# Products that nothing reads in the routing, and another order of two squares in the head

## The chip, the cores and the metric

One core of a Trainium2 chip runs the whole program in one launch. Its engines work side by side, each through its own list of instructions in order, and wait for each other on semaphores: TensorE (PE) multiplies matrices, VectorE (DVE), ScalarE (ACT) and GpSimd (POOL) work element by element, SyncE (SP) issues most of the DMAs. The metric is device time in microseconds (us). TensorE runs at one of two clock levels, 2.4 GHz or 1.2 GHz, which the profile's rows show as a granted clock of 1.00 or 0.50.

## The reference

The input x has 512 rows of 1024. Two blocks follow each other, all in float32:

```python
x = first_block(x, c, ...)      # gated linear attention and pooling, then hier_moe
return second_block(x, ...)     # a gated delta rule layer, swiglu, a stick-breaking attention, swiglu

def hier_moe(h, w_rg, w_re, w_e_in, w_e_out):
    t = h.reshape(-1, D)
    pg = softmax(t @ w_rg)                      # 4 groups: the best one
    gp, gi = top_k(pg, 1)
    le = (t @ w_re).reshape(-1, 4, 8)           # 8 experts in that group: the best two
    le = take_along_axis(le, gi)
    ew, ei = top_k(softmax(le), 2)
    weights = gp * ew / sum(ew)
    ...                                         # 32 experts: y = sum of weight * (silu(t wi_a) * (t wi_u)) @ wo
    return y

# end of first_block, start of second_block
x = x + gt_m * hier_moe(modulate(rmsnorm(x, norm2_g), sh_m, sc_m), ...)
x = rmsnorm(x, final_norm_g)
hn = rms_norm(x, attn_norm[0])
proj = hn @ w_in                                # gdn_mixer: q, k, v, z, b, a
```

gt_m, sh_m and sc_m are columns of silu(c) @ w_ada + b_ada. In gdn_mixer the projected q, k and v go through a short convolution and silu; then, in chunks of 64 rows, a triangular system is solved for each head.

## The kernel before

The data stand transposed: xT has 8 tiles of 128 features by 512 rows. A product of full precision is made of three: the operand is split into a high and a low part (ah and al, by ACT and DVE), the weight as well (whi by ACT, wlo by DVE or POOL), and ah*whi, al*whi and ah*wlo are summed (the function mm3). Every instruction goes through one helper, so all rows of the profile name line 231; they are told apart by the names of their tiles.

**The routing** (moe, lines 1305 to 1500 or so) chooses experts for every row. PE makes small products: with sel (which expert each row has), to count and rank the rows (tile names lA<-sel,lsr); with oh, a one-hot matrix, to list for each pair of experts which rows belong to it (lA<-vals,oh). Between them DVE makes a long chain of small operations, one after the other. From the list DVE makes indices, POOL gathers the rows by indirect DMA, DVE scales them (moex<-moex,sums, the function scaled), PE transposes them (lA<-cst,moex), ACT and DVE modulate them (operand), and the expert products (mm<-slot,moex) begin. In the gaps of this chain the code puts the last two column blocks of the ada product (mm<-wraw,sil, then lC<-cst,ms to turn the row into columns, which DVE adds into modT and modP). The generator gate_gen (lines 1340 to 1350) makes these in steps, and the code calls go(n), n steps, at chosen places: go(4) ahead of everything, go(2) after the products with sel, go(1) after the indices, go(100) after the gathers were issued. Ahead of the expert loop stands a block that runs only if some expert has more rows than its place holds; its branch reads a number that DVE made (line 1622).

**The head** (lines 1721 to 1745) joins the last experts' results into xT, tile by tile (k from 0 to 7), and starts the next stage's first projection two tiles behind. Per tile: PE transposes the experts' results (lA<-to,ylast), DVE adds them into xT, ACT makes ah, DVE makes al, and two sums of squares are kept for two norms: st1, of x, with DVE's addition nacc<-nacc,nsq, and st2, of x times a gain, with POOL's addition of the same name. The helper norm_add (lines 638 to 647) issues the square on ACT and the addition behind it at once. In the program's order ACT makes ah of tile k, the square of st1 for tile k-1, and the square of st2 for tile k; DVE makes xT of k, the addition of k-1, and al of k:

```python
into_x(ps, k)                                          # DVE xT
s.nc.scalar.activation(hh[:, k], x, AF.Copy, ...)      # ACT ah
if k:
    s.norm_add(st1, s.xT[:, k - 1])                    # ACT nsq, DVE nacc, of the tile before
V.scalar_tensor_tensor(out=hl[:, k], ...)              # DVE al
s.norm_add(st2, x, fg[:, k:k + 1], G)                  # ACT nsq, POOL nacc
```

Behind the head PE sums the two norms over the partitions (lA<-nacc,ones), ACT makes R from them, DVE Rc, and each projected piece is scaled by Rc into xm.

**The stage after it** (gdn, from line 1747) is written as generators: projections, convolution (kF, qF, vf: DVE adds three shifted products to one of ACT's), silu on ACT, transposes on PE (lC<-cst,vf), and the triangular solve on DVE, in which 30 steps of a product sub<-mt and an addition mt<-mt,sub follow each other. A planner decides the order in which the generators' steps are emitted: it keeps an emulated time for every engine, from costs written into the program, and asks which lane has work that an engine could start. The times run on from what was emitted in the head, so another order there gives it another start.

Of the kernel before, what the change touches and what calls it, by code (L numbers as in the profile page):

```python
# [12 lines left out]
F = mybir.dt.float32  # L13
# [381 lines left out]
class Kern:  # L395
# [242 lines left out]
    def norm_add(s, st, x, scale=1.0, eng=None):  # L638
        n = st["n"]
        if st["first"]:  # L640
            s.nc.scalar.activation(st["acc"][:, :n], x, AF.Square, scale=scale)
            st["first"] = False
        else:
            q = s.tp.tile([P, 512], F, name="nsq", tag="nsq", bufs=2)
            s.nc.scalar.activation(q[:, :n], x, AF.Square, scale=scale)
            (eng or s.nc.vector).tensor_tensor(out=st["acc"][:, :n], in0=st["acc"][:, :n], in1=q[:, :n], op=OP.add)

# [659 lines left out]
    def moe(s):  # L1307
# [32 lines left out]
        def gate_gen():  # L1340

            for j in (10, 11):
                ps = s.mm_tile()
                for _ in s.ada_gen(j, ps):
                    yield
                ms = s.tp.tile([P, 256], F, name="ms", tag="hF", bufs=2)
                S.activation(ms, ps[:, 0:256], AF.Copy)
                yield
                for _ in s.columns_gen(j, ms):
                    yield  # L1350
# [3 lines left out]
        go(4)  # L1354
        Rt = sm("Rt2", [4])
# [100 lines left out]
        with s.aside():  # L1456
# [3 lines left out]
            skip_runtime_bounds_check_because="the result of a comparison: 0 or 1")  # L1460
        tp_ = s.la_tile([P, 5, NP])
# [195 lines left out]

        warm = sm("warm", [1])
# [47 lines left out]
    def head(s, part, into_x):  # L1706
# [9 lines left out]
        first = [s.mm_tile() for _ in range(2)]  # L1716
        for k in range(KT + 2):
            if k < KT:
                ps = part(k)
                x = s.xT[:, k]  # L1720
                with s.aside():
                    into_x(ps, k)
                    s.nc.scalar.activation(hh[:, k], x, AF.Copy, scale=fag[:, k:k + 1])
                    if k:
                        s.norm_add(st1, s.xT[:, k - 1])
                    V.scalar_tensor_tensor(out=hl[:, k], in0=x, scalar=fag[:, k:k + 1], in1=hh[:, k].bitcast(F),
                                           op0=OP.mult, op1=OP.subtract)
                    s.norm_add(st2, x, fg[:, k:k + 1], G)
                    if k == KT - 1:
                        s.norm_add(st1, x)  # L1730
# [792 lines left out]
```

## Time and profile before

| | us |
|---|---|
| median of 3 runs | 2022.58 (2020.38 to 2023.29) |
| profiled execution | 2029.18 |
| its span in the profile | 2027.4 |
| PE busy | 1949.6, 96% of the span |
| DVE, ACT, POOL busy | 981.0, 756.3, 373.8 |
| mean granted clock of TensorE | 0.973 |

The profile is of one execution; the span leaves out some time around it, and the runs are timed without a profile. A row of a timeline gives start and duration; in brackets stand the idle time of the engine just before and the work whose end released it. Consecutive instructions of one engine and kind are one row with their count (x32); a float32 product counts as two records. The stretches of this program are, in us from the span's start: the first block's mixer up to 325, the routing to 348, the experts to 604.5, the head to 637, the delta rule layer to 1041, and then the rest.

### The profile page before, as it was taken

What the parts mean: (1) busy time and instruction counts of PE and PEld (TensorE: products, weight loads), DVE (VectorE), ACT (ScalarE), POOL (GpSimd) and SP (SyncE); (2) the same over time, 40 slices, a digit from 0 to 9 for tenths busy, and PEclk for the clock granted to TensorE, in tenths of its full rate; (3) what the DMA queues carried; (4) which work ended last, traced back from release to release, by engine and by line L of the source; (5) the groups of instructions that cost most, each with busy time, mean ns of one, the idle gap of its engine ahead of it and who ended that gap; (6) DMA issues with size and microseconds to landing.
All of it is one profiled execution on the core that took longest, in us unless ns stands there. A gap on an engine that the chain in (4) does not pass through costs nothing.

```text
span 2027.4 us, 26781 instructions
## 1 busy us (share of the span) xinstructions
PE 1949.6 (96%) x10717; PEld 1468.5 (72%) x10717; DVE 981.0 (48%) x1612; ACT 756.3 (37%) x1188; POOL 373.8 (18%) x305
## 2 busy tenths in 40 slices
PE   7999997999998997999999999999999989999999
PEld 4776775444445776888788888888888768888887
DVE  3445344334446788545554433445665554433432
ACT  3443322222225653444343312234666542322322
POOL 0513202111105442122121101101221221100110
PEclk8988997999998998999999999999999999999999
DMA  8213286999962323111223333323211123323322
GB/s 300 90 45 115 74 297 224 419 411 401 410 246 57 110 79 96 45 27 42 94 85 94 102 94 94 104 83 104 73 63 58 47 73 104 94 94 97 95 89 73
DMA packets 175367, 268.86 MB, mean 133 GB/s; under 512 B 24300, under 2 KB 148456, under 8 KB 162696
## 3 DMA queue, kind: packets, MB, share of 16 engines
q1 hardware_dynamic: 152784, 249.28, 35.6%
q10 hardware_dynamic: 19784, 13.40, 2.3%
q0 software_dynamic: 2672, 4.44, 0.6%
q8 instruction: 86, 1.41, 0.3%
q14 instruction: 41, 0.34, 0.1%
HBM read 263.41 MB, written 7.86 MB: 134 GB/s over the span
## 4 chain that ended last, share of the span: by engine, by line
PE 73%; DVE 5%; ACT 2%; issue 2%; POOL 1%; DMA 0%; ACTq 0%; POOLq 0%; DVEq 0%
PE mm L231 57%; PE lA L231 9%; PE lB L231 7%; DVE sub L231 1%; DVE xT L231 1%; PE lC L231 1%; DVE qF L231 1%; DVE mt L231 0%; ACT ah L231 0%; DVE kF L231 0%; POOL wlo L231 0%; DVE vf L231 0%; DVE wlo L231 0%; DVE al L231 0%; ACT whi L231 0%
## 5 line engine op out<-in xcount | busy, mean ns | idle before, releaser
L231 PE MATMUL mm<-ah,whi 128*128 128x512 f32 (+1 forms) x1232 | 502.8, 408 | 0.8 <-DVE xT L231 0.4
L231 PE MATMUL mm<-al,whi 128*128 128x512 f32 (+1 forms) x1232 | 487.5, 396 | 7.4 <-DVE al L231 7.3
L231 PE MATMUL mm<-ah,wlo 128*128 128x512 f32 (+1 forms) x1232 | 487.1, 395 | 0.8 <-DVE wlo L231 0.8
L231 DVE TENSOR_TENSOR wlo<-wraw,whi 128x1024 fp32r<-128x1024 f32 (+3 forms) x174 | 216.4, 1245 | 295.6 <-ACT whi L231 293.7
L231 ACT ACTIVATE whi<-wraw 128x1024 fp32r<-128x1024 f32 (+2 forms) x212 | 214.8, 1015 | 331.6 <-PE mm L231 178.6
L231 PEld LDWEIGHTS mm<-ah,whi 128*128 128x128 f32 (+1 forms) x1232 | 233.7, 190 | 61.1 <-issue 11.0
L231 PEld LDWEIGHTS mm<-al,whi 128*128 128x128 f32 (+1 forms) x1232 | 234.2, 190 | 57.8 <-DVE al L231 9.8
L231 PEld LDWEIGHTS mm<-ah,wlo 128*128 128x128 f32 (+1 forms) x1232 | 233.7, 190 | 54.1 <-DVE wlo L231 2.0
L231 POOL TENSOR_TENSOR sg<-sg,fR 128x512 f32<-128x512 f32 x44 | 57.0, 1296 | 525.6 <-ACT sg L231 525.6
L231 POOL TENSOR_TENSOR wlo<-wraw,whi 128x1024 fp32r<-128x1024 f32 x38 | 93.1, 2451 | 254.6 <-ACT whi L231 247.4
L231 PE MATMUL mm<-hidh,whi 128*128 128x512 f32 x352 | 139.2, 395 | 0.0
L231 PE MATMUL mm<-hidh,wlo 128*128 128x512 f32 x352 | 138.0, 392 | 0.0
L231 PE MATMUL mm<-hidl,whi 128*128 128x512 f32 x352 | 136.6, 388 | 0.0
L231 PE MATMUL mm<-slot,moex 128*32 128x512 f32 (+1 forms) x1024 | 117.9, 602 | 0.1
L231 ACT ACTIVATE moex<-lA,modP,g2P 128x128 f32<-128x128 f32 x64 | 27.6, 456 | 161.4 <-PE lA L231 146.0
L231 PEld LDWEIGHTS mm<-slot,moex 128*32 128x32 f32 x1024 | 31.7, 111 | 72.3 <-issue 64.7
L231 PEld LDWEIGHTS mm<-hidh,wlo 128*128 128x128 f32 x352 | 66.1, 188 | 15.5
L231 PEld LDWEIGHTS mm<-hidl,whi 128*128 128x128 f32 x352 | 66.1, 188 | 14.5
L231 PEld LDWEIGHTS mm<-hidh,whi 128*128 128x128 f32 x352 | 66.2, 188 | 13.0
L231 DVE TENSOR_TENSOR xT<-mm,xT 128x512 f32<-128x512 f32 x64 | 44.0, 687 | 55.6 <-PE mm L231 49.7
L231 ACT ACTIVATE hidh<-fu 128x512 fp32r<-128x512 f32 x44 | 27.8, 633 | 103.9 <-DVE fu L231 103.9
L231 DVE TENSOR_SCALAR moex<-lA,g2P,modP 128x128 f32<-128x128 f32 x64 | 25.3, 410 | 85.1 <-ACT moex L231 85.1
(552 smaller groups left out, 3115.4 us busy)
## 6 DMA issues: line engine op xcount, KB each, us to landing
slot<-in_w_e_in_dram SPq DMA_DIRECT2D x64, 1024.0 KB, 11.8
wraw<-in_w_gu_dram SPq DMA_DIRECT2D x88, 512.0 KB, 3.4
slot<-in_w_e_out_dram SPq DMA_DIRECT2D x32, 1024.0 KB, 13.0
wraw<-in_w_down_dram SPq DMA_DIRECT2D x40, 512.0 KB, 3.4
wraw<-in_w_ada_dram SPq DMA_DIRECT2D x32, 512.0 KB, 4.1
wraw<-in_gdn_w_in_dram SPq DMA_DIRECT2D x32, 512.0 KB, 3.8
wraw<-in_w_kv_dram SPq DMA_DIRECT2D x16, 512.0 KB, 3.4
wraw<-in_w_in_dram SPq DMA_DIRECT2D x14, 512.0 KB, 4.6
```

The lines of the kernel that those rows point to most:

```text
L231: r = f(*a, **k)
```

## The change

Three things are changed.

- gate_gen holds back the last step of column block 10 (the turning into columns is done, DVE's addition waits) until the first quarter of block 11's products has been issued, and one more go(1) puts that quarter ahead of the products with oh.
- A function busy(n) makes n products of the ones matrix (128x128, float32) with itself into a PSUM tile that nothing reads: 14 after go(4), 3 ahead of the products with oh, 5 ahead of the expert loop.
- In the head a new function square issues a square on ACT and hands back the addition, to be issued later. ACT now makes ah, the square of st1 and the square of st2, all of tile k; the addition of st1 for tile k is issued in tile k+1, between ah and al. The rest of the program stays, except that the planner gives the stage after the head another order.

```diff
--- before.py
+++ after.py
@@ -644,6 +644,18 @@
             q = s.tp.tile([P, 512], F, name="nsq", tag="nsq", bufs=2)
             s.nc.scalar.activation(q[:, :n], x, AF.Square, scale=scale)
             (eng or s.nc.vector).tensor_tensor(out=st["acc"][:, :n], in0=st["acc"][:, :n], in1=q[:, :n], op=OP.add)
+
+    def square(s, st, x, scale=1.0, eng=None):
+
+        n = st["n"]
+        if st["first"]:
+            st["first"] = False
+            s.nc.scalar.activation(st["acc"][:, :n], x, AF.Square, scale=scale)
+            return lambda: None
+        q = s.tp.tile([P, 512], F, name="nsq", tag="nsq", bufs=2)
+        s.nc.scalar.activation(q[:, :n], x, AF.Square, scale=scale)
+        return lambda: (eng or s.nc.vector).tensor_tensor(out=st["acc"][:, :n], in0=st["acc"][:, :n],
+                                                          in1=q[:, :n], op=OP.add)
 
     def rsqrt_(s, out, src, scale):
         s.nc.scalar.activation(out, src, AF.Ln, scale=scale, bias=s.eps)
@@ -1339,19 +1351,33 @@
 
         def gate_gen():
 
+            last = None
             for j in (10, 11):
                 ps = s.mm_tile()
                 for _ in s.ada_gen(j, ps):
                     yield
+                    if last:
+                        next(last)
+                        last = None
+                        yield
                 ms = s.tp.tile([P, 256], F, name="ms", tag="hF", bufs=2)
                 S.activation(ms, ps[:, 0:256], AF.Copy)
                 yield
-                for _ in s.columns_gen(j, ms):
-                    yield
+                last = s.columns_gen(j, ms)
+                next(last)
+                yield
+            next(last)
+
+        def busy(n):
+
+            ps = s.la_tile(lane="B")
+            for _ in range(n):
+                PE.matmul(ps[:, 0:P], s.ones, s.ones, start=True, stop=True)
 
         gg = gate_gen()
         go = lambda n=1: [next(gg, None) for _ in range(n)]
         go(4)
+        busy(14)
         Rt = sm("Rt2", [4])
         s.rsqrt_(Rt, p2[:, :, 0], 1.0 / D)
         lg = sm("lg", [4, 36])
@@ -1458,6 +1484,8 @@
         _, dyn = nc.values_load_multi_w_load_instructions(
             moi[0:1, 0:NP], engines=[ET.PE], min_val=0, max_val=1,
             skip_runtime_bounds_check_because="the result of a comparison: 0 or 1")
+        go(1)
+        busy(3)
         tp_ = s.la_tile([P, 5, NP])
         for i in range(2):
             h = slice(4 * i, 4 * i + 4)
@@ -1655,6 +1683,7 @@
                 ts_(out=over_, in0=over_, scalar1=-128.0, scalar2=0.0, op0=OP.add, op1=OP.max)
         s.aloof = False
 
+        busy(5)
         warm = sm("warm", [1])
         S.activation(warm, s.eps, AF.Silu)
         s.pairs.room += 1
@@ -1714,6 +1743,7 @@
         hh, hl = s.act_tiles()
         st1, st2 = s.norm_begin(), s.norm_begin()
         first = [s.mm_tile() for _ in range(2)]
+        add = lambda: None
         for k in range(KT + 2):
             if k < KT:
                 ps = part(k)
@@ -1721,13 +1751,13 @@
                 with s.aside():
                     into_x(ps, k)
                     s.nc.scalar.activation(hh[:, k], x, AF.Copy, scale=fag[:, k:k + 1])
-                    if k:
-                        s.norm_add(st1, s.xT[:, k - 1])
+                    add()
                     V.scalar_tensor_tensor(out=hl[:, k], in0=x, scalar=fag[:, k:k + 1], in1=hh[:, k].bitcast(F),
                                            op0=OP.mult, op1=OP.subtract)
-                    s.norm_add(st2, x, fg[:, k:k + 1], G)
+                    add = s.square(st1, x)
                     if k == KT - 1:
-                        s.norm_add(st1, x)
+                        add()
+                    s.square(st2, x, fg[:, k:k + 1], G)()
             if k > 1:
                 kk = k - 2
                 if kk % 4 == 0:
```

PE's list in the routing, before, behind the ada products of block 10 (mm<-wraw,sil), from the products with sel to the last ada products:

```order
L231 MATMUL lA<-sel,lsr 128x128
L231 MATMUL lA<-sel,lsr 128x96
L231 MATMUL lA<-sel,lsr 128x64
L231 MATMUL lA<-sel,lsr 128x32 x5
L231 MATMUL lC<-cst,ms 128x2 x4
L1458 TENSOR_LOAD moi
L231 MATMUL lA<-vals,oh_2666 128x80 x4
L231 MATMUL lA<-vals,oh_2672 128x80 x4
L231 MATMUL mm<-wraw,sil 32x256 x16
```

and now (lB is the tile that nothing reads, TENSOR_LOAD moi reads the flags for the expert loop):

```order
L231 MATMUL lB_2506<-ones 128x128 x14
L231 MATMUL lA<-sel,lsr 128x128
L231 MATMUL lA<-sel,lsr 128x96
L231 MATMUL lA<-sel,lsr 128x64
L231 MATMUL lA<-sel,lsr 128x32 x5
L231 MATMUL lC<-cst,ms 128x2 x4
L1484 TENSOR_LOAD moi
L231 MATMUL mm<-wraw,sil 32x256 x4
L231 MATMUL lB_2687<-ones 128x128 x3
L231 MATMUL lA<-vals,oh_2692 128x80 x4
L231 MATMUL lA<-vals,oh_2698 128x80 x4
L231 MATMUL mm<-wraw,sil 32x256 x12
```

Four of the sixteen last ada products moved ahead of the products with oh, and two groups of products with ones stand in between.

ACT's list at the end of the head, before, from ah of the seventh tile (k = 6) to the load of the table for R:

```order
L231 ACTIVATE ah<-xT,fag 128x512
L231 ACTIVATE nsq<-xT 128x512
L231 ACTIVATE nsq<-xT,vaT 128x512
L231 ACTIVATE whi<-wraw 128x1024
L231 ACTIVATE ah<-xT,fag 128x512
L231 ACTIVATE nsq<-xT 128x512
L231 ACTIVATE nsq<-xT,vaT 128x512
L231 ACTIVATE nsq<-xT 128x512
L218 ACT_TABLE_LOAD
```

and now:

```order
L231 ACTIVATE ah<-xT,fag 128x512
L231 ACTIVATE nsq<-xT 128x512
L231 ACTIVATE nsq<-xT,vaT 128x512
L231 ACTIVATE whi<-wraw 128x1024
L231 ACTIVATE ah<-xT,fag 128x512
L231 ACTIVATE nsq<-xT 128x512
L231 ACTIVATE nsq<-xT,vaT 128x512
L218 ACT_TABLE_LOAD
```

The two kinds of squares (nsq<-xT for st1, nsq<-xT,vaT for st2) stand alike in both. Before, the one for st1 is of the tile before the ah above it, and the last tile's follows at the end; now both are of the same tile as that ah.

DVE's list in the solve, before, from the scaled piece xm to the first vf (the convolution of v), over the fifth to the eighth pair of sub and mt:

```order
L231 TENSOR_TENSOR xm<-mm,Rc 128x512
L231 TENSOR_TENSOR sub<-mt 128x130
L231 TENSOR_TENSOR mt<-mt,sub 128x26x5
L231 TENSOR_TENSOR sub<-mt 128x150
L231 TENSOR_TENSOR mt<-mt,sub 128x25x6
L231 TENSOR_TENSOR sub<-mt 128x168
L231 TENSOR_TENSOR mt<-mt,sub 128x24x7
L231 TENSOR_TENSOR sub<-mt 128x184
L231 TENSOR_TENSOR mt<-mt,sub 128x23x8
L231 TENSOR_SCALAR qss<-lC 128x4
L231 TENSOR_SCALAR qss<-qss 128x4
L231 SCALAR_TENSOR_TENSOR vf<-xm,vbT,vf 128x512 x2
```

and now, over the same pairs:

```order
L231 SCALAR_TENSOR_TENSOR vf<-xm,vbT,vf 128x512
L231 MEMSET xm 128x3
L231 TENSOR_TENSOR xm<-mm,Rc 128x512
L231 TENSOR_TENSOR sub<-mt 128x130
L231 TENSOR_TENSOR mt<-mt,sub 128x26x5
L231 TENSOR_TENSOR sub<-mt 128x150
L231 TENSOR_TENSOR mt<-mt,sub 128x25x6
L231 TENSOR_TENSOR sub<-mt 128x168
L231 TENSOR_TENSOR mt<-mt,sub 128x24x7
L231 TENSOR_TENSOR sub<-mt 128x184
L231 TENSOR_TENSOR mt<-mt,sub 128x23x8
L231 SCALAR_TENSOR_TENSOR vf<-xm,vbT,vf 128x512 x2
```

The first vf, which stood after the eighth pair, now stands after the fourth, and the pairs of vf that follow are one addition further on.

## Rows read from the trace of the kernel before

**Rows 1.** The page: busy time by engine; the chain that ended last.

```profile
PE 1949.6 (96%) x10717; PEld 1468.5 (72%) x10717; DVE 981.0 (48%) x1612; ACT 756.3 (37%) x1188; POOL 373.8 (18%) x305
...
PE 73%; DVE 5%; ACT 2%; issue 2%; POOL 1%; DMA 0%; ACTq 0%; POOLq 0%; DVEq 0%
```

**Rows 2.** Stretch, length, busy of PE, PEld, DVE, ACT, POOL; clock, DMA share, GB/s.

```profile
348.00:604.50 256.50, 255.07 (x1927) 108.04 (x1928) 104.32 (x188) 67.10 (x129) 37.93 (x28) 0.99 0.94 381
...
604.50:632.50 28.00, 20.00 (x70) 13.29 (x68) 18.55 (x24) 17.13 (x27) 15.08 (x9) 0.90 0.13 34
...
737.00:800.00 63.00, 48.53 (x239) 38.70 (x239) 57.14 (x105) 19.53 (x25) 24.67 (x12) 0.89 0.30 82
```

**Rows 3.** Timeline, PE, routing: start, duration, products, [idle before, releaser].

```profile
325.96 1.93 PE L231 MATMUL mm<-wraw,sil 128*32 128x256 f32 x32
...
332.82 1.86 PE L231 MATMUL lA<-sel,lsr 128*128 128x128 f32 x8 [4.92 <-DVE sel L231]
...
338.56 1.90 PE L231 MATMUL lA<-vals,oh 128*128 128x80 f32 x8 [2.20 <-DVE oh L231]
...
340.39 3.55 PE L231 MATMUL mm<-wraw,sil 128*32 128x256 f32 x32
...
348.02 1.95 PE L231 MATMUL lA<-cst,moex 128*128 128x128 f32 x8 [2.45 <-DVE moex L231]
```

**Rows 4.** Stretches of the routing: length, busy PE, clock, DMA share, GB/s.

```profile
331.00:343.00 12.00, 7.98 (x52) 0.50 0.70 251
...
348.00:353.50 5.50, 5.48 (x28) 0.50 0.88 294
```

**Rows 5.** Timeline, PE, further on: products of 128x128 at full clock.

```profile
692.96 1.95 PE L231 MATMUL lB<-kF 128*128 128x128 f32 x16
```

**Rows 6.** Timeline, POOL and DVE, routing: first gather, scaling of gathered rows.

```profile
341.17 1.13 POOL L1491 DMA_INDIRECT moex<-x1d,src  x1 [5.02 <-DVE tk L231]
...
347.12 0.75 DVE L231 TENSOR_SCALAR moex<-moex,sums 128x1024 f32<-128x1024 f32 x1 [1.35 <-DVEq L1622]
```

**Rows 7.** Timeline, DVE, head.

```profile
608.10 0.75 DVE L231 SCALAR_TENSOR_TENSOR al<-xT,fag,ah 128x512 fp32r<-128x512 f32 x1 [0.79 <-ACT ah L231]
...
623.37 0.75 DVE L231 SCALAR_TENSOR_TENSOR xT<-lA,modT,xT 128x512 f32<-128x512 f32 x1
...
625.43 0.69 DVE L231 TENSOR_TENSOR nacc<-nacc,nsq 128x512 f32<-128x512 f32 x1 [1.31 <-ACT nsq L231]
...
626.70 0.74 DVE L231 SCALAR_TENSOR_TENSOR xT<-lA,modT,xT 128x512 f32<-128x512 f32 x1
...
628.75 2.05 DVE L231 TENSOR_TENSOR nacc<-nacc,nsq 128x512 f32<-128x512 f32 x1 [1.31 <-ACT nsq L231]
...
630.72 1.75 DVE L231 SCALAR_TENSOR_TENSOR al<-xT,fag,ah 128x512 fp32r<-128x512 f32 x1
```

**Rows 8.** Timeline, ACT and PE, head.

```profile
624.78 0.61 ACT L231 ACTIVATE nsq<-xT 128x512 f32<-128x512 f32 x1
...
636.77 0.69 ACT L231 ACTIVATE R<-lA,eps 128x512 f32<-128x512 f32 x1 [4.01 <-PE lA L231]
...
634.83 3.09 PE L231 MATMUL lA<-nacc,ones 128*128 128x512 f32 x4
```

**Rows 9.** Timeline, POOL, head.

```profile
609.28 1.29 POOL L231 TENSOR_TENSOR nacc<-nacc,nsq 128x512 f32<-128x512 f32 x1 [17.45 <-ACT nsq L231]
...
627.89 2.36 POOL L231 TENSOR_TENSOR wlo<-wraw,whi 128x1024 fp32r<-128x1024 f32 x1
...
630.21 1.72 POOL L231 TENSOR_TENSOR nacc<-nacc,nsq 128x512 f32<-128x512 f32 x1
```

**Rows 10.** Timeline, PE and DVE, solve of the next stage.

```profile
775.84 1.11 PE L231 MATMUL lC<-cst,vf 128*128 128x128 f32 x4 [8.88 <-ACT vf L231]
...
769.05 1.41 DVE L231 SCALAR_TENSOR_TENSOR vf<-xm,vbT,vf 128x512 f32<-128x512 f32 x2
...
774.38 1.41 DVE L231 SCALAR_TENSOR_TENSOR vf<-xm,vbT,vf 128x512 f32<-128x512 f32 x2
```

## The prediction

> **What bounds the kernel now.** I read the page first. TensorE is busy for 96% of the span, and the chain that ended last lies on PE for 73% of its length [rows 1]. A change can therefore give time back only where PE stands still or works at its lower clock. Next I read busy time by stretch [rows 2]. The expert products (348 to 604.5) keep PE busy 255.07 of 256.5 us; the head (604.5 to 632.5) only 20.00 of 28; the triangular solve of the next stage (737 to 800) 48.53 of 63, with DVE at 57.14. Then I read the timelines of the routing (325 to 354), the head and the solve engine by engine, and the granted clock beside them. All sums are in the profiled execution's own time, 2029.2 us (span 2027.4 and 1.8 around it), which is 6.6 us above the median of the runs, 2022.6.
>
> **Routing.** PE works until 327.89, waits 4.92 for the selection and 2.20 for the one-hot matrix, makes 32 records of the ada product and waits 2.45 before the first transpose [rows 3]. The clock shows 0.50 from 331 to 343 and again from 348 to 353.5 [rows 4], each time after PE had idled. The same 32 ada records take 3.55 at 0.50 and 1.93 at full clock [rows 3].
>
> The change adds 22 products of 128x128. Sixteen records of such a shape (8 products) take 1.95 at full clock [rows 5], 0.24 a product; 22 make 5.4 us, twice that at the lower clock. The first 14 end near 327.9 + 3.4 = 331.3, before the selection is ready at 332.82, so they cost nothing. Four of the ada products (8 records, 0.48 at full clock) and three of the new ones (0.72) go in front of the vals,oh products, 1.2 us of work, or 2.4 at the lower clock, in the hole of 2.20: at worst +0.2 (and as much again if the weights of these four land late, for which I have no row; together +0.3). The last five lie after the branch, where PE idled 2.45 before the transposes [rows 3].
>
> What this can give is three things. The vals,oh products took 1.90 at 0.50, so half of that, 0.95, goes at full clock, less the fill; the gathers start when DVE has made the indices from them (341.17) and the scaling of the gathered rows at 347.12 waits for gather and branch [rows 6]. I take 0.8 of it. The first transposes, 1.95, lose up to 0.9. The first expert records behind them, from 349.97, run at 0.50 until at least 353.5 [rows 4] and would lose half of those 3.5 us, 1.8. The ada products themselves end earlier too (12 behind vals,oh, not 16), but the scaling at 347.12 was the later end. All together 3.5 at best, +0.3 at worst. PE worked from 338.56 on and was still at 0.50 until 343, so products need not lift the clock at once, and the idle gap before the transposes shrinks but does not go. I take -2.0, nearer to the middle than to either end. The expert stretch then has to pass this on: its PE is 99% busy, and no wait on a slot shows, so I count it whole; if the slot loads were the bound, it would be nil.
>
> **Head.** For every tile DVE makes xT, the sum of squares of the tile before (nacc) and the low part al. In steady state a tile takes 3.33 us (xT at 623.37, next at 626.70), and in each DVE waits 1.31 for ACT's square, because ACT made that square, of the tile before, only after this tile's ah [rows 7]. In the first tiles, without a sum, DVE waits 0.79 for ah before al, and that is all: 0.66 + 0.79 + 0.75 = 2.2 a tile [rows 7]. In the changed order the square of tile k-1 is done before xT of tile k. DVE's order stays, so the 0.69 of nacc falls into the 0.79 in which al waits for ah anyway. ACT's work per tile stays at three operations like the square's 0.61 [rows 8], about 2.0 a tile, and PE needs ten products of 0.23, 2.3 a tile. That would give 2.3 a tile.
>
> Something is late next, though. POOL's own sum (nacc of the second norm) starts when ACT's last square of the tile ends, now just when DVE wants its nacc. It takes 1.29 at 609.28 but 1.72 at 630.21 beside DVE's al; and DVE's nacc at 628.75 took 2.05 instead of 0.69, ending only after POOL's wlo (627.89 + 2.36); the al behind it took 1.75 instead of 0.75 [rows 7, 9]. So the two exclude each other, and whoever comes second waits. If POOL's sum always comes first, the tile takes xT 0.66 + 1.29 + nacc 0.6 + al 0.65 = 3.2; if never, 2.3. I take the middle, 2.75. From the fourth xT to the eighth that is four tiles by 0.58, 2.3 us.
>
> By the Trainium skill, "SBUF — State Buffer", section "Who interferes with whom", a DVE instruction with two SBUF inputs and a GpSimd instruction that reads SBUF take one port pair as an exclusive lock, and issue order decides who blocks. This trace agrees (2.05 beside 2.36); the rule speaks against the change, because it makes the two sums ask together, and by it alone the tile would stay at 3.2.
>
> In the last tile, xT at 626.70 is followed by an al that ends at 632.47, 5.77 later: 1.31 for the square, then the stretch behind POOL's wlo and POOL's sum. Now nacc can start right behind xT, before ACT's whi has let POOL begin wlo, so al ends some 3.2 after its xT: 2.5 less (if wlo comes first all the same, nothing of it). PE's last five products and the ones products of the norms, 3.09 at a clock of about half, follow, and R on ACT at 636.77 [rows 8]. They still need POOL's wlo (2.36) and last sum (1.72), which I place at about 626 to 628.4 and to 630.1, so that R falls near 632. Head: -2.3 - 2.5 = -4.8, of which I take -4.5 for POOL's tail. Bounds: -1.0 (tiles keep 3.2, only the last gains) and -7.0 (2.3 a tile and no collision).
>
> **The stage after the head.** Its order is emitted by a planner that starts from the emulated end of the head, and it comes out differently. PE waits 8.88 at 775.84 for vf, which rests on the fifth vf of DVE at 774.38 [rows 10]. In the new order that vf stands where the pair of 769.05 stood, with one more vf ahead: 5.33 - 0.7 = 4.6 earlier. Against it, between the first sub and the clearing of mt DVE has 8 vf instead of 6, 6 qF instead of 5, and one xm more: four by 0.70 (1.41 for two [rows 10]), 2.8 later for the end of the solve, which the work behind it may feel. I take -0.5, near nothing, since DVE sets the pace there; bounds -4 and +5, the second being the extra 2.8 and a new wait of some 2.
>
> **Sum.** -2.0 - 4.5 - 0.5 = -7.0: 2022.2 in the profiled execution's time, 2015.6 against the median. The starting place of everything behind shifts with it, since PE is 96% busy there.
>
> **Rivals.**
> - The tiles run at PE's pace: 2.3 a tile, head -7, with the clock up early in the routing, -3. Total about -11: 2011.5. For it: ACT and DVE have room by their durations. Against it: 2.05 at 628.75.
> - The lock decides: POOL's sum always comes first and the routing clock falls as before. Head -1 to -2, routing -0.5, total about -2: 2020.5. For it: both sums are released by the same ACT sequence each tile.
> - Slot loads or gathers take the routing's gain: head alone, -4.5 to -5: 2018. Against it: no slot wait of PE.
> - The other side: the new order in the solve. DVE is busy 57.14 of 63 there; if its 2.8 us more push the end of the solve and a wait like that 8.88 forms again further on, behind another late vf or qF, it costs 2.8 + 8.9 = 11.7. That is more than 7.0 from the point at which the new wait exceeds 4.2. Total +4.7: 2027.3.
> - The fill does nothing and the squares are hidden: no change, 2022.6.
>
> **How the numbers follow.** Forecast (-4.1 to -10) 0.53; PE's pace 0.09; head alone 0.10, half of it beyond 4.1; lock 0.12; no change 0.05; other side 0.11 (of which 0.09 beyond +4.1). A measurement of this kernel tells 0.2% (4.1 us) from no change. Faster 0.53 + 0.09 + 0.05 = 0.67, and I give 0.03 of it away for the planner's order, whose bounds are the widest: 0.64. Slower is 0.09 and 0.02 of these, 0.11; the rest is the same, 0.25. The range for 8 in 10: 2008.5 (-14, all good bounds together) to 2023.0 (a little over no change). The forecast's own range is 2012 to 2018.5.
>
> **What would show it.** Routing right: granted clock above 0.6 from 333 to 343 and PE at full clock on the first expert records before 351. Wrong: 0.50 there, or vals,oh starting later than 338.8. Head right: xT about 2.7 apart, DVE's nacc waiting on no ACT square, R 4 to 5 us earlier relative to the first xT. Wrong: xT still 3.2 or more apart, with nacc stretched to over 1.2 beside POOL. Stage behind: the wait for vf near 4 instead of 8.88; wrong if PE's waits between 737 and 860 sum to more than before. The forecast fails if head and routing gain and the stretch 640 to 860 grows by as much.

## The result and the profile after

The change makes the kernel slower. After: 2039.58 us, median of 4 runs (2036.56 to 2043.35); before: 2022.42 (4 runs, 2020.38 to 2023.29). The ratio is 1.0082 [1.0062, 1.0102]. The time lies above the predicted range, on the side that had 0.11.

The page of after, busy time by engine and the chain that ended last:

```profile
PE 1965.3 (96%) x10761; PEld 1482.8 (73%) x10761; DVE 987.3 (48%) x1612; ACT 753.9 (37%) x1186; POOL 372.6 (18%) x305
...
PE 72%; DVE 5%; issue 2%; ACT 2%; POOL 1%; DMA 0%; ACTq 0%; DVEq 0%; POOLq 0%
```

PE is busy 15.7 us longer than before [rows 1], though the 22 added products (44 records) are worth 5.4 at full clock. The profiled span grew by 14.2, to 2041.6. Laid out between instructions that both traces have, the difference is: first block, where both lists are the same, +3.0; routing and experts, up to the first xT of the head, -0.3; head, first xT to R, -4.0; R to the first sub of the solve, +3.9; solve, to the clearing of mt, +3.7; from there, through the scan over the chunks, to the first product of the layer's output (mm<-mh), +6.7; all behind it, +1.2. So the head gained and the stage after it lost 14.3.

**Routing.** Timelines of after, PE and then DVE (start, duration, records, idle before and its releaser):

```profile
330.87 3.39 PE L231 MATMUL lB<-ones 128*128 128x128 f32 x28
335.85 1.15 PE L231 MATMUL lA<-sel,lsr 128*128 128x128 f32 x8 [1.59 <-DVE sel L231]
...
341.79 1.91 PE L231 MATMUL lA<-vals,oh 128*128 128x80 f32 x8
...
350.77 2.51 PE L231 MATMUL lB<-ones 128*128 128x128 f32 x10 [1.97 <-DVEq L1650]
353.07 1.39 PE L231 MATMUL lA<-cst,moex 128*128 128x128 f32 x8
```

```profile
351.00 0.75 DVE L231 TENSOR_SCALAR moex<-moex,sums 128x1024 f32<-128x1024 f32 x1 [1.35 <-DVEq L1650]
```

Windows of PE (stretch, length, busy, records, granted clock, DMA share, GB/s):

```profile
337.00:346.50 9.50, 8.62 (x54) 0.50 0.77 253
350.50:353.50 3.00, 2.73 (x13) 0.50 0.88 277
```

The products with sel run at full clock now (1.15 for what took 1.86 in [rows 3]), but those with oh still take 1.91 and the clock is 0.50 again from 337, without a long idle time ahead. The last five fill products wait for the same branch as the transposes and take 2.51 at half clock; the scaled rows (DVE, 351.00 + 0.75) were ready at 351.75, but the transposes start at 353.07, 1.3 later; before, they started 0.15 after the rows (347.87 and 348.02) [rows 3, 6].

**Head.** Timelines of after, DVE, POOL and ACT:

```profile
618.30 0.75 DVE L231 SCALAR_TENSOR_TENSOR xT<-lA,modT,xT 128x512 f32<-128x512 f32 x1
618.96 1.76 DVE L231 TENSOR_TENSOR nacc<-nacc,nsq 128x512 f32<-128x512 f32 x1
...
621.30 0.74 DVE L231 SCALAR_TENSOR_TENSOR xT<-lA,modT,xT 128x512 f32<-128x512 f32 x1
621.97 1.49 DVE L231 TENSOR_TENSOR nacc<-nacc,nsq 128x512 f32<-128x512 f32 x1
...
624.04 0.74 DVE L231 SCALAR_TENSOR_TENSOR xT<-lA,modT,xT 128x512 f32<-128x512 f32 x1
...
626.78 0.74 DVE L231 SCALAR_TENSOR_TENSOR xT<-lA,modT,xT 128x512 f32<-128x512 f32 x1
...
628.86 2.83 DVE L231 SCALAR_TENSOR_TENSOR al<-xT,fag,ah 128x512 fp32r<-128x512 f32 x1
```

```profile
618.87 1.30 POOL L231 TENSOR_TENSOR nacc<-nacc,nsq 128x512 f32<-128x512 f32 x1 [2.84 <-ACT nsq L231]
621.62 1.29 POOL L231 TENSOR_TENSOR nacc<-nacc,nsq 128x512 f32<-128x512 f32 x1 [1.45 <-ACT nsq L231]
...
628.36 2.79 POOL L231 TENSOR_TENSOR wlo<-wraw,whi 128x1024 fp32r<-128x1024 f32 x1
```

```profile
635.45 0.69 ACT L231 ACTIVATE R<-lA,eps 128x512 f32<-128x512 f32 x1 [4.46 <-PE lA L231]
```

The last tiles are 2.74 apart instead of 3.33 [rows 7], and nacc waits for no square. POOL's sum starts ahead of it, by 0.1 to 0.35 us, and beside POOL's 1.30 DVE's sum takes 1.76 or 1.49, where it took 0.69 at 625.43 in [rows 7]. The last al meets POOL's wlo in the same way (2.83 beside 2.79) and ends 4.91 after its xT.

**The stage after the head.** Waits of PE from 604 to 1060 (us in total, times, longest), before and then after:

```profile
PE lC L231 <- ACT vf L231: 8.9, 1, 8.9
...
PE lC L231 <- ACT cs L231: 7.2, 3, 3.3
...
PE lA L231 <- POOL gS L231: 0.6, 1, 0.6
```

```profile
PE lC L231 <- ACT cs L231: 15.5, 7, 7.0
...
PE lA L231 <- POOL gS L231: 3.1, 1, 3.1
PE lC L231 <- ACT vf L231: 2.8, 1, 2.8
PE lB L231 <- DMA inverted<-inv: 2.2, 1, 2.2
```

cs are the squares of k and q whose sums give the norms of a head; gS is the state that the scan carries over the chunks; inverted is the solved system, which comes back through a DMA. The wait for vf shrank as forecast, 8.88 to 2.78, but a wait for cs of 7.00 took its place, and two smaller ones, of 3.12 and 2.24, stand in the scan. Timeline of PE, after, over the solve and the scan:

```profile
671.07 1.00 PE L231 MATMUL lC<-ones,cs 128*64 128x2 f32 x16 [2.34 <-ACT cs L231]
...
773.16 0.81 PE L231 MATMUL lC<-cst,vf 128*128 128x128 f32 x4 [2.78 <-ACT vf L231]
...
795.20 1.02 PE L231 MATMUL lC<-ones,cs 128*64 128x2 f32 x16 [7.00 <-ACT cs L231]
...
843.78 1.16 PE L231 MATMUL lA<-gS,wq 128*128 128x128 f32 x8 [3.12 <-POOL gS L231]
...
865.47 1.84 PE L231 MATMUL lB<-inverted,XTs 128*128 128x128 f32 x8 [2.24 <-DMA inverted<-inv]
```

The cs of the long wait is made from a late qF, which ACT itself had waited for (ACT's timeline, after):

```profile
793.38 0.63 ACT L231 ACTIVATE qF<-qF 128x512 f32<-128x512 f32 x1 [10.68 <-DVE qF L231]
...
794.53 0.61 ACT L231 ACTIVATE cs<-qF 128x512 f32<-128x512 f32 x1
```

POOL's timeline, after and then before, where the state is cleared:

```profile
840.92 2.34 POOL L231 TENSOR_TENSOR wlo<-wraw,whi 128x1024 fp32r<-128x1024 f32 x1 [3.43 <-ACT whi L231]
843.21 0.52 POOL L231 MEMSET gS<- 128x512 f32 x1
```

```profile
835.67 2.36 POOL L231 TENSOR_TENSOR wlo<-wraw,whi 128x1024 fp32r<-128x1024 f32 x1 [3.95 <-ACT whi L231]
837.97 0.53 POOL L231 MEMSET gS<- 128x512 f32 x1
```

The clearing takes half a us and depends on nothing, but POOL works in order, and it stands behind a wlo that waits for ACT's whi. Counted from R, the clearing ends 6.5 us later than before (at 208.3 instead of 201.7), and PE comes to the scan's first product (lA<-gS,wq) only 4.0 later (at 205.2 instead of 201.2). So it waits 3.12 instead of 0.57.

Windows of PE over the same 55 us of the scan, counted from R + 200, before and then after:

```profile
836.80:891.80 55.00, 52.70 (x406) 1.00 0.10 20
```

```profile
835.50:890.50 55.00, 48.87 (x324) 0.88 0.10 20
```

After gets through 324 records in the time of 406: PE stands 3.8 us more, and the granted clock falls to 0.50 for parts of it.

Windows of PE from the first sub to mm<-mh, before and then after:

```profile
753.42:971.12 217.70, 202.19 (x1313) 0.98 0.19 52
```

```profile
756.01:984.07 228.06, 210.17 (x1314) 0.94 0.18 49
```

PE makes the same products in both. Of the 10.4 us more, 2.4 are time in which PE stands, and 8.0 are work that takes longer at the lower clock.

### The profile page after: what moved, and what is told of

Its sections match the earlier page's. It is cut to its first block, busy times and chain, and to the rows that moved or that the text cites. A ratio compares the mean times of both kernels' runs of the same rounds, so it can differ in the third digit from the quotient of the medians.

```text
span 2041.6 us, 26874 instructions
## 1 busy us (share of the span) xinstructions
PE 1965.3 (96%) x10761; PEld 1482.8 (73%) x10761; DVE 987.3 (48%) x1612; ACT 753.9 (37%) x1186; POOL 372.6 (18%) x305
## 4 chain that ended last, share of the span: by engine, by line
PE 72%; DVE 5%; issue 2%; ACT 2%; POOL 1%; DMA 0%; ACTq 0%; DVEq 0%; POOLq 0%
PE mm L231 56%; PE lA L231 9%; PE lB L231 7%; DVE kF L231 1%; DVE qF L231 1%; DVE mt L231 1%; PE lC L231 1%; DVE sub L231 1%; DVE xT L231 1%; ACT whi L231 0%; DVE nacc L231 0%; POOL wlo L231 0%; DVE wlo L231 0%; ACT ah L231 0%; ACT nsq L231 0%
## 5 line engine op out<-in xcount | busy, mean ns | idle before, releaser
L231 PEld LDWEIGHTS mm<-slot,moex 128*32 128x32 f32 x1024 | 31.5, 110 | 70.5 <-issue 63.6
```

What stands on the lines that cost most here:

```text
L231: r = f(*a, **k)
```

## The experiments

Most kernels replay an order of the stage after the head: the planner's choices were written down as a list PLAN (which lane makes how many steps at each call; lane J is the solve, A the scan) and are followed instead of made:

```diff
     def tick(s):
+        if s.follow():
+            return
...
     K.moe()
+    K.script = [list(zip(c[::2], map(int, c[1::2]))) for c in PLAN.split(',')]
     K.gdn()
+    K.script = None
```

In the table, x is the start of the head's first xT, R ACT's R, sub the first sub of the solve, mt the MEMSET of mt behind it, mh the first product of the layer's output. The times are from one profile each; "sum" is x to mh, against before's 366.8; the scan's column is PE's busy time and mean clock from R + 200 to R + 255; the ratio is of timed runs against before.

| kernel | x-R | R-sub | sub-mt | mt-mh | sum | scan | ratio [95%] |
|---|---|---|---|---|---|---|---|
| before | 32.4 | 116.7 | 41.7 | 176.0 | 0 | 52.70, 1.00 | 1 |
| after | 28.4 | 120.6 | 45.3 | 182.7 | +10.2 | 48.87, 0.88 | 1.0082 [1.0062, 1.0102] |
| e1_old_order | 28.3 | 120.6 | 42.1 | 176.1 | +0.3 | 52.09, 1.00 | 1.0004 [0.9984, 1.0024] |
| e2_new_order | 31.9 | 116.1 | 46.0 | 181.5 | +8.7 | 49.28, 0.88 | 1.0063 [1.0041, 1.0085] |
| e3_new_early | 28.4 | 120.5 | 41.3 | 180.1 | +3.5 | 52.38, 0.94 | 1.0037 [1.0020, 1.0054] |
| e4_new_late | 28.9 | 116.9 | 46.4 | 182.5 | +7.9 | 48.44, 0.88 | 1.0042 [1.0023, 1.0061] |
| e5_solve_as_before | 28.3 | 120.5 | 40.2 | 193.4 | +15.6 | 48.52, 0.87 | 1.0051 [1.0026, 1.0076] |
| e6_solve_as_after | 28.2 | 120.7 | 46.4 | 178.4 | +6.9 | 52.47, 0.91 | 1.0024 [1.0003, 1.0046] |
| e7_head_alone | 28.5 | 116.5 | 42.2 | 176.0 | -3.6 | 52.69, 1.00 | 0.9988 [0.9965, 1.0010] |
| e8_swap | 26.3 | 120.6 | 42.1 | 176.1 | -1.7 | 52.06, 1.00 | 0.9969 [0.9949, 0.9990] |
| e9_gs_early | 28.4 | 119.2 | 46.0 | 176.2 | +3.0 | 52.38, 0.91 | 0.9980 [0.9957, 1.0003] |
| e10_scan_fill | 28.5 | 119.1 | 46.1 | 181.0 | +7.9 | 51.04, 0.91 | 1.0027 [1.0003, 1.0050] |
| e11_gs_late | 28.5 | 119.4 | 41.9 | 188.2 | +11.2 | 48.40, 0.81 | 1.0055 [1.0034, 1.0076] |
| e12_head_swap | 26.4 | 120.8 | 42.1 | 176.0 | -1.5 | 52.07, 1.00 | 0.9961 [0.9936, 0.9985] |
| e13_fill_at_cs | 25.9 | 117.8 | 42.1 | 181.6 | +0.6 | 52.45, 0.91 | 0.9999 [0.9979, 1.0019] |
| e14_swap_gs | 26.0 | 116.1 | 41.7 | 178.3 | -4.7 | 53.27, 0.94 | 0.9983 [0.9960, 1.0006] |
| e15_before_gs | 31.5 | 116.7 | 42.1 | 179.1 | +2.6 | 53.67, 0.91 | 1.0033 [1.0016, 1.0050] |
| e16_swap_gs_own | 25.9 | 117.8 | 46.2 | 172.6 | -4.2 | 52.65, 1.00 | 0.9978 [0.9962, 0.9995] |

The sum and the ratio do not agree in size, and for e9 not in direction (+3.0 in its profile, -0.20% in its runs): what lies outside x to mh differs from one execution to the next with the same instructions. The first block, whose lists are the same in all 18 kernels, ends (first ada product of the routing) at 316.3 to 319.8 us in eight of the profiles and at 322.5 to 331.8 in ten; in those ten the clock is at 0.50 for over 10 us between 172 and 196, in the eight it is not. The ratios of e1 and of e3 to e16 rest on 10 to 12 runs each (after 4, e2 6), and runs of one kernel spread by up to 19 us. Each ratio is against before's runs of its own series. Before's median was 2024.8 to 2029.3 in the later series, above the 2022.4 of the first, and after was not timed again: against those later medians its 2039.58 is 0.5 to 0.7% longer.

**The order, alone and undone.** e1 is after with before's list; e2 is before with after's list. One line of the list, before's and after's:

```diff
-    "1,,I1,B1W1,C1V1,C1,,W1,I1C1V1,V1,B1J1V1W1,V1,V1W1,C1,C1W1,C1W1,C1W1,C1,J1C1V1,J1C1V1,,W1,W1,,,J1C1,V"
+    "1C1,C1W1,I1,V1,V1W1,W1,C1V1W1,C1V1W1,,B1J1C1,V1,V1W1,C1W1,C1W1,C1W1,C2,J1C1V1,C1V1,J1C1,V1,W1,W1,,,J"
```

> The whole change, but the delta rule stage after the head is emitted in the order that the kernel before has (its planner's choices are written out as a list and followed). Theory (the new order of that stage costs some 14 us, the head gives 4, the last five products in the routing cost 1 to 2): 2018 to 2021, two or three us under before; R after the first xT of the head still 28.4 us. Rival (the loss lies ahead of the stage: 3 us in the first block, the products with ones and the clock levels that they shift): it stays above 2030.

> The kernel before, untouched in routing and head, with the delta rule stage in the changed kernel's order. Theory (the order is what costs): 2034 to 2038, 12 to 15 over before. Rival (the order costs only because the stage starts at another phase of clock and loads, or nothing): within 4 us of before.

e1 takes the loss away and leaves no gain; e2 has the loss without the head or the fill. The order is the cause. It costs 0.63% by e2; by the medians of after and e1, which come from different series, it costs 11.9 us, 0.6%. In e1's profile the head's 4.0 came to nothing: R to sub is 3.9 longer than in before.

**Which half of it.** e3 follows after's list up to a point (inside the solve) where both orders have emitted the same work, then before's; e4 is the reverse.

```diff
-    "1C1,C1W1,I1,V1,V1W1,W1,C1V1W1,C1V1W1,,B1J1C1,V1,V1W1,C1W1,C1W1,C1W1,C2,J1C1V1,C1V1,J1C1,V1,W1,W1,,,J"
+    "1C1,C1W1,I1,V1,V1W1,W1,C1V1W1,C1V1W1,,B1J1C1,V1,V1W1,C1,C1W1,C1W1,C1W1,C1,J1C1V1,J1C1V1,,W1,W1,,,J1C"
```

> The whole change; the delta rule stage in the new order up to the last k and first q projections, from there (the solve and what stands beside it) in the old order; at the seam both orders have done the same work. If the loss comes from the solve on: as e1_old_order, 2018 to 2021. If it comes from the early part (first sub 2.6 us later): 2024 or more.

> The whole change; the old order up to the same seam, the new one from there. If the loss comes from the solve on: 2032 to 2037. If from the early part: under 2024.

The late half carries the longer solve, the gS wait (3.1) and the clock of 0.88. The early half is not free; it has no such wait (gS 0.6), but its scan is at 0.94. By the runs the two halves cost alike (0.37 and 0.42%), so the loss is not in the late half alone, and what makes e3 slower is not shown.

**The solve's place.** e5 is after with its own list, only the solve's steps (J) where before has them; e6 is e1 with the solve's steps where after has them.

```diff
-    "1,V1,W1,,,,J1,V1,V2,C1W1,C1V1,,,J1,,,W1,C1W2,C1V1W1,C1,,J1,V1,W1C1J1V1V2,C1,V1W1,C1V1,J1C1,W1,V1W2,J"
+    "1,V1,W1,,,,J1,J1V1,V2,C1W1,C1V1,J1,,,,,J1W1,C1W2,C1V1W1,C1,,,J1V1,W1C1V1V2,C1,V1W1,J1C1V1,C1,W1,V1W2"
```

> The changed kernel with its own new order in the delta rule stage, except that the solve's steps (sub, mt) are emitted at the places where the kernel before has them, ahead of some vf and qF on DVE; PE's list is that of the changed kernel, word for word. Theory (the new order lets convolution steps go ahead of the solve, whose later end makes PE wait for gS, kd and the inverted blocks at a lower clock): the first sub to the clearing of mt back from 45.3 to about 42, PE's wait for gS from 3.1 to under 1, R to the first mh product 339 to 343 instead of 348.6, the run about 2030 to 2034. Rival (the order of PE's own list, or of the projections, is what costs): 347 to 349 and 2038 to 2041.

> The reverse: the whole change with the old order (as e1_old_order), but the solve's steps at the later places of the new order; PE's list as in e1_old_order. Theory: sub to mt 44 to 46 instead of 42.1, waits for gS and the inverted blocks come back, R to mh 343 to 348 instead of 338.8, the run 2031 to 2036. Rival: as e1_old_order in each stage, within 1 us.

My first theory, the solve's end, falls with e5: the solve is 5 us shorter and the layer longer than in after. In e6's profile a late solve has a price all the same (sum +6.6 over e1); the runs do not show it, since the intervals of e6 and e1 overlap.

**The clearing of gS.** e9 is after with its own list, and the state cleared ahead of everything else of the layer; e11 is e1 (old order, no wait) with the clearing made eight times as long; e10 is after with 13 unread products ahead of the first product with gS.

```diff
-        states = {}
+        states = {0: t4("gS", 2)}
+        G.memset(states[0], 0.0)
...
-            if t == 0:
+            if t == 0 and g:
                 states[g] = t4("gS", 2)
```

> The changed kernel with its own order, word for word, on PE, DVE, ACT and SP; only POOL clears the scan's first state gS ahead of the stage instead of behind a wlo. e5_solve_as_before has refuted that the solve's end is what PE waits for. New theory: PE comes to the scan's first product before POOL has done the wlo that stands ahead of the clearing, waits 3.1, and the clock falls behind that wait (R + 210 to 216.5, and again at 230 and 247). Without the wait: no wait for gS, no stretch at 0.50 between R + 205 and R + 220, R to the first mh product 341 to 345 instead of 348.6, the run 2030 to 2036 where the changed kernel takes 2040. Rival (the wait only holds back what waits for something else right after, wlo or the inverted blocks): 347 to 349.

```diff
                 p1 = bank()
+                if n == 0 and c == 0:
+                    for _ in range(13):
+                        PE.matmul(p1[:, 0], s.ones, s.ones, start=True, stop=True, skip_group_check=True)
```

> The changed kernel with its own order; 13 more products of ones with ones (3.1 us at full clock), which nothing reads, ahead of the scan's first product, in PE's wait for gS. If the price of that wait is mostly the clock behind it: the wait stays (shorter, with the products in it), but 0.50 from R + 210 to 216.5 is gone, R to mh 3 less, 344 to 346. If the clock falls there anyway, from the small products of the scan themselves: 348 to 350.

```diff
                 states[g] = t4("gS", 2)
-                G.memset(states[g], 0.0)
+                for _ in range(1 if g else 8):
+                    G.memset(states[g], 0.0)
```

> The whole change with the old order (as e1_old_order), but POOL clears gS eight times in a row, 3.6 us more, so that PE has to wait for it as in the changed kernel. Theory (this wait and the clock behind it are most of the loss in the scan): wait for gS about 4, a stretch at 0.50 behind it, R to mh 343 to 348 instead of 338.8. Rival (the wait is made good later): 338 to 341.

PE's timelines of the first product with gS in e9 and in e11:

```profile
824.76 1.05 PE L247 MATMUL lA<-gS,wq 128*128 128x128 f32 x8
```

```profile
831.52 2.07 PE L247 MATMUL lA<-gS,wq 128*128 128x128 f32 x8 [4.66 <-POOL gS L247]
```

In e9 only the clearing moved in POOL's list: mt to mh falls from 182.7 to 176.2, and the loss is gone from the runs: the slowest of e9's twelve (2031.8) lies below the fastest of after's four (2036.6). In the profile x to mh is still 3.0 over before, with a solve as long as after's. In e11 a wait of 4.66, put into the good order, makes the loss: clock 0.81, mt to mh 188.2 where e1 has 176.1, +0.55% where e1 has +0.04%. That is more than the wait itself, and PE's other waits in the scan are no longer than in e1. The fill (e10) covers the wait (0.2 is left) and gets back part: mt to mh 181.0, +0.27%.

e15 is the caveat: before with the same early clearing.

> The kernel before with nothing but POOL's clearing of gS ahead of the stage. Theory (the old order hardly waits for it): within 0.1% of before. If it is 0.3% faster, the clearing weighs on the old order too, and e9_gs_early's gain says less about the new one.

It has even less to wait for than before, yet is 0.33% slower. Its first product with gS and its scan, from PE's timeline and windows:

```profile
832.49 1.05 PE L247 MATMUL lA<-gS,wq 128*128 128x128 f32 x8
...
830.90:885.90 55.00, 53.67 (x383) 0.91 0.10 20
```

PE is busier than in before (53.67 against 52.70), but gets through 383 records instead of 406, because the clock falls without a wait of more than 0.8. Both kernels have a wait of 0.56 some 216 us after R; behind it the clock stays at 1.00 in before and falls to 0.50 in e15. e14, further down, repeats this on top of e12: mt to mh 178.3 instead of 176.0, at 0.94. So the wait for gS is enough to bring the loss (e11), but taking it away does not settle the clock. What decides it when no wait is left, stays open.

**The head alone, the squares swapped, the gain that did not come.** e7 is before with the head's edit and before's list, no fill. e8 is e1 with the two squares exchanged on ACT and without busy(5); e12 is before with the head's edit so exchanged, routing untouched.

```diff
                     V.scalar_tensor_tensor(out=hl[:, k], ...)
+                    s.square(st2, x, fg[:, k:k + 1], G)()
                     add = s.square(st1, x)
                     if k == KT - 1:
                         add()
-                    s.square(st2, x, fg[:, k:k + 1], G)()
```

> Only the squares' new order in the head; routing as before, old order in the delta rule stage. First xT to R 28.4 instead of 32.4. What e1_old_order showed (from R to the first sub 3.9 more, by a wait of PE for cs at about R + 36 and a stretch at the lower clock behind it) tells two theories apart: if the head's gain is always eaten there, R to first sub is 120 to 121 and the run is within 1.5 us of before; if that hung on how the clock's fall met the waits, as in e4_new_late (116.9), it is 116 to 118 and the run 3 to 4 faster.

> As e1_old_order, but ACT makes the square of the second norm ahead of that of the first, so that POOL starts its sum earlier and meets DVE's al rather than its nacc; and the five products ahead of the expert loop are left out. If the lock between DVE's and POOL's sums is what keeps a tile at 2.74: xT to xT 2.2 to 2.5, first xT to R 26 to 27.5 instead of 28.3. If ACT or PE sets it: 2.7 as before. Without the five products the first transposes start 1.0 to 1.2 after the scaling of the gathered rows begins instead of 2.1, but at the lower clock: ada to first expert product 25.4 to 26 instead of 26.6.

> A version meant to beat both: the kernel before with the old order written out, routing untouched, and in the head ACT's order ah, square of the second norm, square of the first, of the same tile. e8_swap had first xT to R 26.3, so 6 less than before. If the stage behind gives nothing back (R to first sub 116 to 117, as in e7_head_alone): 0.2 to 0.4% under before, 5 to 8 us. If it eats 4 as in e1_old_order and e8_swap (120.6): 1 to 3 us under before.

e7 keeps the head's gain in its profile: R to sub is 116.5, and the sum is 3.6 under before. Its runs do not tell it from before (0.9988 [0.9965, 1.0010]).

DVE's and then POOL's timeline of e12 in the head:

```profile
617.45 0.74 DVE L247 SCALAR_TENSOR_TENSOR xT<-lA,modT,xT 128x512 f32<-128x512 f32 x1
618.11 1.12 DVE L247 TENSOR_TENSOR nacc<-nacc,nsq 128x512 f32<-128x512 f32 x1
...
619.81 0.74 DVE L247 SCALAR_TENSOR_TENSOR xT<-lA,modT,xT 128x512 f32<-128x512 f32 x1
```

```profile
617.27 1.41 POOL L247 TENSOR_TENSOR nacc<-nacc,nsq 128x512 f32<-128x512 f32 x1 [0.96 <-ACT nsq L247]
```

With st2's square first, POOL's sum is more than half done when DVE wants its own: nacc 1.12 instead of 1.49 to 1.76, tiles 2.36 apart, and the head another 2 us shorter. e12 and e8 beat before, by 0.39 and 0.31%, and with it after.

The next question is where the head's gain goes. e13 is e12 with ten unread products ahead of the wait for cs behind the head.

```diff
+            if ss is kss and h == 2:
+                idle = s.la_tile()
+                for _ in range(10):
+                    PE.matmul(idle[:, 0:P], s.ones, s.ones, start=True, stop=True)
             p = bankC([4, 2])
```

> e12_head_swap with ten products of ones with ones, which nothing reads, ahead of the third group of products that wait for cs (some R + 34 to 36, where PE waits 2.4 in the kernels with the short head). Theory (the head's gain is given back there: PE comes too early for cs, waits 2.4, and the stretch at 0.50 behind the wait costs some 3 more): no 0.50 from R + 36 to 42.5, R to the first sub 117 to 118 instead of 120.8, the run 2 to 4 us under e12_head_swap. Rival (DVE's chain to the first sub sets the time whatever PE does): 120 to 121.

The windows of PE around that place, in before and in after:

```profile
661.50:668.00 6.50, 6.07 (x28) 0.50 0.22 53
671.50:677.50 6.00, 6.00 (x55) 1.00 0.31 87
```

```profile
661.00:664.00 3.00, 3.00 (x9) 0.50 0.00 0
671.50:677.50 6.00, 6.00 (x26) 0.50 0.07 22
```

In after PE waits a second time for cs (2.34 at 671.07) and falls to 0.50 behind it, 26 records where before has 55. The 18 profiles split on this second wait, some 34 to 36 us after R. Ten have one of 2.3 to 4.1 us, and R to sub is 119.1 to 120.8 in them; the other eight have none, or 0.9 (e16), and R to sub is 116.1 to 117.8. Among the eight are e4, e7 and e14, which have a short head too, and e4 has e1's lists up to here, where e1 is one of the ten. In e4 the clock is at 0.50 behind the first wait for cs, 25 us after R, and stays there for 6 us, much as in before; the later group that waits 2.41 in e1 does not wait. PE's timeline and window of e4:

```profile
664.22 0.98 PE L247 MATMUL lC<-ones,cs 128*64 128x2 f32 x16 [2.85 <-ACT cs L247]
...
674.29 0.63 PE L247 MATMUL lC<-ones,cs 128*64 128x2 f32 x16
```

```profile
664.50:670.50 6.00, 6.00 (x26) 0.50 0.30 72
```

So the short head alone does not decide whether its gain is passed on; when the clock falls, in the single execution, goes with it, and what decides that is not shown. With the fill (e13) R to sub is 117.8 instead of e12's 120.8, but that is one profile, and kernels without the fill reach it as well. In the same profile the scan lost more than that (clock 0.91, mt to mh +5.6), and the runs are level with before (0.9999). e12's runs gained some 8 us on before, its profile only 1.5.

**Both together.** e14 is e12 with the early clearing; e16 is e14 without a list, its planner choosing for itself.

```diff
-    K.script = [list(zip(c[::2], map(int, c[1::2]))) for c in PLAN.split(',')]
     K.gdn()
-    K.script = None
```

> e12_head_swap with POOL's clearing of gS ahead of the stage. In the old order PE waits only 0.57 for gS, so R to mh goes down by 0.5 to 1 and the run is within 2 us of e12_head_swap, unless the clock falls less often in the scan.

> As e14_swap_gs, but the planner orders the stage by itself, as it would in use. Theory (with the clearing out of POOL's way, an order of the planner's choice costs little): R to mh 336 to 343, the run within 4 us of e14_swap_gs. Rival (each new order has some such wait): 345 or more, and 5 to 12 us slower than e14_swap_gs.

e16 is faster than before (0.22%) without a fixed order; neither beats e12. e16's solve is as long as after's (46.2), but mt to mh is 172.6, so a long solve alone does not make the loss.

## Why the prediction was wrong

**The step that failed** is the stage after the head: "I take -0.5, near nothing, since DVE sets the pace there; bounds -4 and +5". It measured +10.4 in the pair of profiles (sub to mh), outside its bounds, and +14.3 counted from R. The terms of that step were one wait of PE, four operations of DVE and, in the upper bound, a new wait of some 2; it had none for the clock: 8.0 of the 10.4 us are PE's products at a mean clock of 0.94 instead of 0.98. The wait for vf did go as said (2.78; forecast 4), but "DVE sets the pace there" stopped at the solve's end. The rival on the other side had the right mechanism for the solve, a new wait behind a late qF in place of the old one (cs, 7.00; solve +3.7), and too little chance; its price of 4.7 in all misses the scan. The sign that was named for it, PE's waits between 737 and 860 summing to more than before, did not come (16.6 before, 16.3 after), so it could not have told the loss.

What I did not compare is POOL's list with PE's at the scan's start: the wait of 0.57 for gS stood in the trace of before, with a wlo and its whi ahead of it, and a PE that comes 2.5 us earlier relative to it turns that into 3.1 and a clock of 0.88. All five kernels with that wait (after, e2, e4, e5, e11) are slower by 0.4 to 0.8%; e11 makes it by itself, e9 removes it. That e3, e6, e10 and e15 are slower without it, by 0.24 to 0.37%, leaves the last part of the mechanism open.

**The head** came out near its forecast: tiles at 2.74 (forecast 2.75), the two sums colliding, R 4.0 earlier (forecast 4.5). In part that was luck. 2.75 was the middle between POOL's sum always first (3.2) and never (2.3); in the trace it is first in each of the last tiles, but only by 0.1 to 0.35, so that DVE waits for the rest of it alone. The tiles gave 2.6 (forecast 2.3), and what follows the last xT gave 1.4 where 2.5 less some 0.3 was put down: its al ended 4.91 after its xT and not 3.2, behind POOL's wlo. The trace agrees once more with the rule of the Trainium skill, "SBUF — State Buffer", section "Who interferes with whom", that a DVE instruction with two SBUF inputs and a GpSimd instruction that reads SBUF contend for one port pair: DVE's sum takes 1.76 beside POOL's 1.30. In e7 and in e12 alike POOL's sum comes first, and DVE's takes 1.49 to 1.76 in e7 and 1.12 in e12, where POOL is further ahead.

What failed is passing the gain on: in after R to sub is 3.9 longer, with a second wait for cs and the half clock behind it. Over the 14 profiles with a short head (e13 left out) R to sub averages 119.2, over the three with a long one 116.5, so 2.7 of the gain is given back on average, though e4, e7 and e14 give back none. "The starting place of everything behind shifts with it" was an assumption, and no row stood for it.

**The routing** was small: between the same rows -0.3 in this pair; over ten profiles with the fill the stretch from the router's products to the first xT averages 278.6, over eight without it 280.0, so about -1.4 (forecast -2.0), with overlapping ranges (277.5 to 279.2 and 278.3 to 281.1). The sign "granted clock above 0.6 from 333 to 343" was not met (0.50 from 337, with everything 3.0 later), and the products with oh start 0.2 later, not earlier (341.79 less 3.0 is 338.8; before 338.56). The five products behind the branch were counted as nothing, since PE idled there, but they wait for the branch too, and some 1.2 of their 2.5 us lies on the path in after. In e9, e10 and e11 they took 1.6 to 1.7 and ended just as the rows came: there the transposes start 0.15 after the rows, as in before.

**The rest of the +17.** The first block, with equal lists, took 3.0 more in the profile, and in e2's profile it took 7.4 less than in before's, where the stretch from 176.5 to 193.5 is at 0.50 (58 records in 17.0 us) against 1.00 in e2 (100). A single profile does not tell such terms from the change; the runs of e1 and e2 do.

## What to carry to other kernels

When an edit makes a planner reorder a later stage, pin the old order first and time the edit with it, and the new order without the edit. Compare every engine's list with that of the engine that bounds, as far as the next place where both meet, small clearings in the queue of a slow engine above all, and try these early: here it took a loss of 0.6% back in one order (e9) and cost 0.33% in another (e15). A stretch that ends earlier may give nothing if the next wait is met earlier too, least of all when the clock falls behind that wait.

## What was not expected of the hardware

A wait of 3 to 5 us in the scan cost more than itself: in e11 4.66 became 12.1 in mt to mh, with the granted clock at 0.81. The clock also fell with PE busy 53.67 of 55 us and no such wait (e15, 0.91), and rested at 1.00 with 52.70 (before). The runs of one kernel, ten or more of them, spread by 10 to 19 us, so that differences of 0.2% needed a dozen runs, and before's median moved by 7 us from one series to another.
